# A hybrid decoder layer on one Trainium2 core: eight operand sums of the second token half moved into the up-projection, the output weight ring in other memory, the first up operands prepared earlier

## The chip, the core and the metric

The kernel runs on one core of one Trainium2 chip. TensorE multiplies (PE in the profile; its weight loads are PEld), VectorE (DVE) and ScalarE (ACT) do elementwise work, GpSimd (POOL) and SyncE (SP) mostly issue DMAs. The metric is the device time of one execution in microseconds, the median of several. Lower is better.

## The reference

One layer, 2048 tokens of width 1024, all in float32. Two token mixers (a gated linear recurrence and an RWKV-7 recurrence) make the rows of `o`; they are untouched by the change. What follows them is:

```
x = x + concat(o_hg, o_rw) @ w_out            # 1024 x 1024
h = rmsnorm(x, norm2_w)
u = h @ w_up                                  # 1024 x 5632
u = causal_depthwise_conv(u, conv_w, width 3) + conv_b
gate, val = split(u)                          # 2816 each
x = x + (silu(gate) * val) @ w_down           # 2816 x 1024
out = rmsnorm(x, final_norm_w)
```

## The kernel before

**Precision and products.** Every float32 operand is split into a high part (a cast by ScalarE, line 237 or 244) and a low part (a subtraction by DVE, line 238 or 245), and one product is three matmuls (`mm3`, lines 260 to 262). The up- and the down-projection each use a scheme with seven block products instead of eight. Its price is that sums and differences of operand blocks have to be made.

**Stages.** Phase 1 does the input projection, the mixers, and the output projection of the token blocks 0 to 2 (512 tokens each). What the change touches comes behind it.

*Output projection of block 3* (lines 1144 to 1219). For two column halves `dh` there are eight steps; a step multiplies one 128-row part of `o` (`take`, operand parts in `Bh[3]`, `Bl[3]`, `Bh[5]`, `Bl[5]`) by one piece of `w_out` (`weights`). The split weights go into a ring of three `woh` and three `wol` tiles. `xh` holds the residual rows of x, four tiles for each `dh` in a ring of six; DVE adds the product to them (line 1218) and SP stores them to `x1d`. In the second half the moving operands 0, 1 and 4 of the up-projection are built beside it (`build`), and its first weights `A0` are loaded. The pool `op` that holds these tiles is opened when phase 1 has given its memory back, so its tiles lie where tiles of phase 1 lay; `yo`, the last result of the RWKV heads, is stored to DRAM by POOL out of such memory.

*Up-projection* (`run`, line 1324). The loop runs over 2 x 22 iterations: token half h (1024 tokens, two blocks), then 22 column blocks. An iteration multiplies seven operands made of the weight quarters a11, a12, a21, a22 by seven moving operands B0 to B6, each product being 12 matmuls: a11 with B0, then (`late`) a22 with B6 and s4 with B2 of the iteration before, then a12 with B1, s2 with B4, s1 with B3, s3 with B5, where s1 = a21 + a22, s2 = s1 - a11, s3 = a11 - a21, s4 = a12 - s2. In iteration 0 the operand parts B3, B5, B6 and B2 are still built, four `build` calls ahead of the product before. Behind the seven products the convolution, SiLU and multiplication make `y`, which SP stores to `gd_` (line 1423): blocks 0 and 1 in half 0, blocks 2 and 3 in half 1.

*Work aside.* A list `side` holds small pieces of other work; after every product `aside(n)` takes one (line 1290). In half 0 these are the second norm of the blocks 2 and 3 and the operand sums for half 1 and for `w_down`; in half 1 the sums for the down-projection of the tokens of half 0: for each of 11 row blocks kk, four loads of `gd_`, four DVE operations (`s_make`), four stores to `Sg[0]`. `four` makes the pieces, with pauses (`None`) in which the loads land. They use the ring `br` of six tiles.

*Down-projection* (lines 1429 to 1519). 143 steps, for each token half g seven products of 11 row blocks (one product of half 0 is made beside the up-projection). A step loads two tiles `draw`, splits them, and does 12 matmuls. The same sums for the second token half (`g_sums`, into `Sg[1]`) are made here: `sums_at` spreads the eleven over the steps 13, 18, 23 to 63. Their first use is at step 88.

**What sets the order.** The program is one list; a scheduler places each engine's instructions by priority and by its own estimate of when operands are ready. On the chip each engine, and SP with its DMA issues, then runs its list strictly in order, each instruction waiting on semaphores. So whatever stands behind a waiting instruction on the same engine waits too.

Of the kernel before, what the change touches and what calls it, by code (L numbers as in the profile page):

```python
# [61 lines left out]
def tile_layer(ctx, tc, consts, x, norm1_w, w_in, hg_lb_logits, hg_norm_w, rw_shift_mu, rw_w0, rw_w2,  # L62
# [1044 lines left out]
    with ExitStack() as c2:  # L1107
# [11 lines left out]
        def raw_(src):  # L1119
            t_ = hr.tile([P, BLK], F32, tag="br", name="br", bufs=6)  # L1120
            if src is not None:
                loader[0](t_, src)
            return t_
# [20 lines left out]
        with tc.tile_pool(name="op", bufs=1, reuse_waits="tile") as op_:  # L1144
# [43 lines left out]
                return wh, wl  # L1188

            xt = {}  # L1190
            for dh in range(2):
                accs = [pst("wacc") for _ in range(4)]
                for n, k in enumerate((0, 1, 4, 5, 2, 3, 6, 7)):
                    w = weights(k, dh)
                    if dh == 0:
                        take(k)
                    if n == 5:
                        for i in range(4):
                            t0 = b * BLK + i * P
                            xt[i] = op_.tile([P, 512], F32, tag="xh", name="xh", bufs=6)  # L1200
                            load(xt[i], x[0, t0:t0 + P, dh * 512:dh * 512 + 512])
                    if dh == 0 and n == 6:
                        rows_of_conv()
                    if dh == 1 and n == 4:
                        for i, (lo_, hi_) in enumerate(((0, 88), (88, 176))):
                            vps = pst("cps")
                            TE.transpose(vps[:, 0:88], crow[i], ident[0:88, 0:88])
                            V.tensor_copy(cvt[:, lo_:hi_], vps[:, 0:88])
                        A0 = up_raw(0)
                    if dh == 1 and 2 <= n:  # L1210
                        for j in range(2):
                            q = 2 * (n - 2) + j
                            build(0, (0, 1, 4)[q // 4], q % 4)
                    for i in range(4):
                        is_ = slice(i * P, (i + 1) * P)
                        mm3(accs[i], (ohl[k][0][:, is_], ohl[k][1][:, is_]), w, n == 0, n == KD - 1)
                for i in range(4):
                    V.tensor_add(xt[i], accs[i], xt[i])
                    dma(x1d[b][i * P:(i + 1) * P, dh * 512:dh * 512 + 512], xt[i])


        with tc.tile_pool(name="up", bufs=1, reuse_waits="tile") as up:
# [2 lines left out]
            V.memset(halo, 0.0)  # L1225


            side = []

            def norm_last(b, i2):  # L1230

                xt = []

                def load():
                    for q in range(2):
                        xt.append(up.tile([P, D], F32, tag="xt2", name="xt2", bufs=2))
# [11 lines left out]
                side.extend([load, None, lambda: scale(0), lambda: scale(1), None] + [lambda: next(g)] * KD)  # L1248

            def four(srcs, make, dsts):  # L1250

                ts = []
                side.extend([lambda: ts.extend(raw_(v) for v in srcs), None,
                             lambda: make(ts, 0), lambda: (make(ts, 1), [dma(d, t_) for d, t_ in dsts(ts)]), None])

            def t_make(ts, part):
                b11, b12, b21, b22 = ts
# [30 lines left out]
            late_side = len(side) - late_side  # L1288
# [18 lines left out]
            def between():  # L1307

                accs = [pst("fa") for _ in range(4)]
                for kk in range(KH):  # L1310
                    lhs, rhs = (split(uw, raw_(v), [P, BLK], "uw", 5)
                                for v in (krows(gd_[0], 1, kk), wd_quarter(1, 0, kk)))
                    for i in range(4):
                        mm3(accs[i], [t_[:, i * P:(i + 1) * P] for t_ in lhs], rhs, kk == 0, kk == KH - 1, True)
                    if kk == KH - 1:
                        break
                    yield
                for i in range(4):
                    t_ = raw_(None)
                    act(t_, accs[i], AF.Copy)  # L1320
                    dma(M2[i], t_)
                yield

            def run():
                fill_ = between()
# [8 lines left out]
                for n in range(2 * NFF + 1):  # L1334
                    h, fb = n // NFF, n % NFF
                    if n < 2 * NFF:
# [42 lines left out]
                    operand("a12", a12)  # L1379
                    prod(acc_b, "a12", 1, True)  # L1380
                    V.tensor_add(cg[:, 2:2 + BLK], acc_b, m1)
                    s1 = up.tile([P, 4, P], F32, tag="s1", name="s1", bufs=1)
                    s2 = up.tile([P, 4, P], F32, tag="s2", name="s2", bufs=1)
                    V.tensor_add(s1, a21, a22)
                    V.tensor_sub(s2, s1, a11)
                    operand("s2", s2)
                    prod(acc_a, "s2", 4, False)
                    m2 = part(acc_a, "m2")
                    operand("s1", s1)
# [39 lines left out]
    with tc.tile_pool(name="dn", bufs=1, reuse_waits="tile") as dn:  # L1429
# [121 lines left out]
```

## Time and profile before

| | |
|---|---|
| median of 3 timed runs | 2756.31 us (2747.66 to 2756.97) |
| the profiled execution | 2742.4 us |
| its span in the profile | 2740.6 us |
| granted TensorE clock | 0.989 of full |
| TensorE busy | 2638.4 us |
| VectorE busy | 1899.1 us |
| ScalarE busy | 1349.5 us |
| read from HBM / written | 376.27 MB / 138.41 MB |
| weight pieces for the up-projection | 176 DMAs of 256 KB |

In the profile, a row of a timeline gives the start, the length, the engine (SPq is the queue of DMA issues of SyncE), the line, the operation and its tiles, a count when equal instructions were merged, and in brackets how long the engine idled before and on whom it waited. A row of waits reads: who waited, for whom, microseconds in total, how many times, the longest. Matmuls overlap, so a 128x512 matmul is shown with about 0.39 us though the next one starts sooner. The input projection and the mixers take the first 1380 us, the output projection of block 3 goes on to 1431, the up-projection to 2331, and the rest is the down-projection.

### The profile page before, as it was taken

The page shows a single profiled execution, that of the slowest core. Times are in us where ns is not written, and L with a number is a line of the kernel's source. Part 1 is how long each engine was busy: PE and PEld are TensorE (multiplying, and loading weights), DVE is VectorE, ACT ScalarE, POOL GpSimd, SP SyncE. Part 2 cuts the span into 40 slices and gives each one's busy share as a digit, 9 for nine tenths or more (in the row PEclk, how much of TensorE's full clock was granted, in tenths as well). Part 3 has the DMA queues.
Part 4 walks back from the last instruction along what each step waited for, and adds up shares of the span by engine and source line. Part 5 has one row for each costly group of instructions (what it writes and reads, how often), then busy time and mean ns, then how long its engine had stood idle before and what let it go on. Part 6 is the DMA issues. An engine that isn't in the chain of part 4 may idle for free.

```text
span 2740.6 us, 47945 instructions
## 1 busy us (share of the span) xinstructions
PE 2638.4 (96%) x18059; PEld 2098.8 (77%) x18059; DVE 1899.1 (69%) x3665; ACT 1349.5 (49%) x2168; POOL 368.9 (13%) x660
## 2 busy tenths in 40 slices
PE   7999999989999999999899999999999999998998
PEld 6777777767777767778677888887888888776887
DVE  4857656575456664757568789988898787667656
ACT  5455443444544444443356754556445554445544
POOL 6433222212222113222100000000000000000000
PEclk9999999999999999999999999999999999999999
DMA  8655544355653546933674467746763222999865
GB/s 303 199 166 166 165 136 130 117 148 183 214 167 111 148 152 204 311 123 119 182 265 139 140 199 258 240 148 207 264 232 113 90 86 76 323 333 327 298 194 184
DMA packets 365437, 517.87 MB, mean 189 GB/s; under 512 B 97439, under 2 KB 194069, under 8 KB 365205
## 3 DMA queue, kind: packets, MB, share of 16 engines
q1 hardware_dynamic: 313265, 345.39, 38.9%
q0 software_dynamic: 51872, 169.41, 19.0%
q8 instruction: 142, 2.33, 0.4%
q14 instruction: 90, 0.74, 0.1%
q10 hardware_dynamic: 68, 0.02, 0.0%
HBM read 376.27 MB, written 138.41 MB: 188 GB/s over the span
## 4 chain that ended last, share of the span: by engine, by line
PE 68%; DMA 10%; DVE 8%; issue 6%; ACT 5%; SPq 1%; POOL 1%; DVEq 0%; ACTq 0%; POOLq 0%
PE pj L260 8%; PE pj L261 7%; PE pj L262 7%; PE ua L262 5%; PE ua L260 5%; PE ua L261 5%; PE ud L262 2%; PE ud L260 2%; PE ud L261 2%; PE da L261 2%; PE da L260 2%; PE da L262 2%; PE hg L971 2%; DMA woraw<-in_w_out_dram 2%; PE ub L262 1%
## 5 line engine op out<-in xcount | busy, mean ns | idle before, releaser
L260 PE MATMUL pj<-hh,wh 128*128 128x512 f32 x960 | 403.5, 420 | 1.4 <-ACT hh L117 0.7
L261 PE MATMUL pj<-hl,wh 128*128 128x512 f32 x960 | 379.5, 396 | 0.0
L262 PE MATMUL pj<-hh,wl 128*128 128x512 f32 x960 | 379.2, 395 | 0.0
L260 PE MATMUL ua<-Bh,uwh 128*128 128x512 f32 x704 | 276.8, 393 | 4.9 <-ACT uwh L244 3.1
L262 PE MATMUL ua<-Bh,uwl 128*128 128x512 f32 x704 | 275.1, 391 | 0.2 <-DVE uwl L245 0.2
L261 PE MATMUL ua<-Bl,uwh 128*128 128x512 f32 x704 | 274.7, 390 | 0.0
L260 PEld LDWEIGHTS pj<-hh,wh 128*128 128x128 f32 x960 | 181.7, 189 | 54.7 <-issue 11.8
L261 PEld LDWEIGHTS pj<-hl,wh 128*128 128x128 f32 x960 | 182.0, 190 | 39.4 <-issue 6.2
L262 PEld LDWEIGHTS pj<-hh,wl 128*128 128x128 f32 x960 | 181.6, 189 | 39.8 <-issue 0.4
L244 ACT CAST uwh<-uraw 128x512 fp32r<-128x512 f32 x220 | 134.1, 617 | 124.6 <-PE ua L261 58.5
L245 DVE TENSOR_TENSOR uwl<-uraw,uwh 128x512 fp32r<-128x512 f32 x220 | 147.0, 686 | 48.7 <-ACT uwh L244 48.5
L244 ACT CAST dah<-draw 128x512 fp32r<-128x512 f32 x140 | 87.0, 622 | 184.7 <-DMA draw<-Sg 60.0
L245 DVE TENSOR_TENSOR dal<-draw,dah 128x512 fp32r<-128x512 f32 x140 | 96.6, 690 | 103.8 <-ACT dah L244 103.5
L260 PEld LDWEIGHTS ua<-Bh,uwh 128*128 128x128 f32 x704 | 132.6, 188 | 33.6 <-ACT uwh L244 3.5
L262 PEld LDWEIGHTS ua<-Bh,uwl 128*128 128x128 f32 x704 | 132.5, 188 | 28.4 <-DVE uwl L245 0.6
L261 PEld LDWEIGHTS ua<-Bl,uwh 128*128 128x128 f32 x704 | 132.7, 188 | 27.0
L260 PE MATMUL ud<-Bh,uwh 128*128 128x512 f32 x352 | 137.9, 392 | 0.3 <-ACT uwh L244 0.3
L262 PE MATMUL ud<-Bh,uwl 128*128 128x512 f32 x352 | 137.1, 390 | 0.0
L261 PE MATMUL ud<-Bl,uwh 128*128 128x512 f32 x352 | 137.0, 389 | 0.0
L261 PE MATMUL da<-dbl,dah 128*128 128x512 f32 x340 | 133.3, 392 | 1.3 <-DVE dbl L245 1.3
L262 PE MATMUL da<-dbh,dal 128*128 128x512 f32 x340 | 132.3, 390 | 0.0
L260 PE MATMUL da<-dbh,dah 128*128 128x512 f32 x340 | 124.6, 392 | 6.5 <-ACT dbh L244 6.5
(570 smaller groups left out, 6050.3 us busy)
## 6 DMA issues: line engine op xcount, KB each, us to landing
uraw<-in_w_up_dram SPq DMA_DIRECT2D x176, 256.0 KB, 3.4
woraw<-in_w_out_dram POOLq DMA_DIRECT2D x96, 256.0 KB, 3.5
draw<-Sg SPq DMA_DIRECT2D x88, 256.0 KB, 3.4
draw<-Tw SPq DMA_DIRECT2D x88, 256.0 KB, 3.4
gd<-y SPq DMA_DIRECT2D x86, 256.0 KB, 3.0
xt<-x1d SPq DMA_DIRECT2D x32, 512.0 KB, 7.2
wraw<-in_w_in_dram POOLq DMA_DIRECT2D x60, 256.0 KB, 4.7
br<-in_w_down_dram SPq DMA_DIRECT2D x58, 256.0 KB, 3.8
```

What stands on the lines that cost most here:

```text
L244: S.copy(hi, src)
L245: V.tensor_sub(lo, src, hi.bitcast(F32))
L260: TE.matmul(acc, lh, rh, start=first, stop=False, skip_group_check=skip)
L261: TE.matmul(acc, lh, rl, start=False, stop=False, skip_group_check=skip)
L262: TE.matmul(acc, ll, rh, start=False, stop=last, skip_group_check=skip)
L971: TE.matmul(o, kt[:, t0:t0 + 64], qs, start=True, stop=True, tile_position=(0, e * 64))
```

## The change

Three edits.

1. *Sums of the second token half.* The list `side` now carries with each piece the first iteration at which it may be taken. Behind the eleven sums of half 0, whose pieces now become free one sum an iteration from iteration 23 on, come the first eight (`EARLY`) of the second half: sum kk from iteration 35 + kk on, the one in which the rows it needs have just been stored. In the down-projection three sums remain, at the steps 13, 19 and 25.
2. *The output weight ring.* The four first `xh` tiles are allocated ahead of the ring, and `xh` gets eight buffers instead of six. The ring `woh`, `wol` so comes to lie in other memory, and `xh` where it lay.
3. *The first up operands.* In iteration 0 a12, s2 and s1 are made and split right behind a11, ahead of the building of B3, B5, B6 and B2. `s1` and `s2` move from the pool `up`, which follows `op` in the same memory, to the pool `uw`.

```diff
+    EARLY = 8
...
+            def x_tile(i):
+                xt[i] = op_.tile([P, 512], F32, tag="xh", name="xh", bufs=8)
+
+            for i in range(4):
+                x_tile(i)
             for dh in range(2):
...
-                            xt[i] = op_.tile([P, 512], F32, tag="xh", name="xh", bufs=6)
+                            if dh:
+                                x_tile(i)
...
-            side = []
+            side, first_at = [], [1]
+
+            def aside_of(fs):
+
+                side.extend((first_at[0], f) for f in fs)
...
-            late_side = len(side)
-            for kk in range(KH):
-                four([krows(gd_[u], q, kk) for u, q in QB], s_make, s_out(lambda i, kk=kk: krows(Sg[0][i], 0, kk)))
+            for g in range(2):
+                for kk in range(({0: KH, 1: EARLY})[g]):
+                    first_at[0] = NFF + 1 + g * (KH + 1 + kk)
+                    four([krows(gd_[2 * g + u], q, kk) for u, q in QB], s_make,
+                         s_out(lambda i, g=g, kk=kk: krows(Sg[g][i], 0, kk)))
...
-                if side and (1 <= n < NFF - 2 or n > NFF) and (n > NFF or len(side) > late_side):
-                    f = side.pop()
+                if side and n >= side[-1][0] and not NFF - 2 <= n <= NFF:
+                    f = side.pop()[1]
...
+            def weight_sums(a11, a21, a22):
+
+                s1, s2 = (uw.tile([P, 4, P], F32, tag=nm, name=nm, bufs=1) for nm in ("s1", "s2"))
+                V.tensor_add(s1, a21, a22)
+                V.tensor_sub(s2, s1, a11)
+                return s1, s2
...
                         if n == 0:
+                            operand("a12", a12)
+                            s1, s2 = weight_sums(a11, a21, a22)
+                            operand("s2", s2)
+                            operand("s1", s1)
                             for kk in range(4):
                                 build(0, 3, kk)
...
-        sums_at = {KH + 5 * j + 2: j for j in range(KH)}
+        sums_at = {KH + 6 * j + 2: EARLY + j for j in range(KH - EARLY)}
```

The line numbers of the changed kernel are one higher from line 181 on, and more further down. How the instructions stand, at three places:

ScalarE's list where the output projection of block 3 begins, before; `uraw` holds the loaded pieces, `woh` are the split weights, `Bh` the operand parts, and the brackets name the semaphores that an instruction waits for (DMASW is a queue of POOL, DMAHW one of SP):

```order
L237 CAST woh<-uraw 128x512 [waits DMAHW0_49,DVE_49]
L237 CAST woh<-uraw 128x512 [waits DMASW0_49,DVE_49,Activation_49]
L237 CAST woh<-uraw 128x512 [waits DMAHW0_49]
L237 CAST Bh_14661<-uraw 128x512 [waits PE_49]
L237 CAST Bh_14661<-uraw 128x512
L237 CAST Bh_14664<-uraw 128x512 [waits DMAHW1_49]
```

and now:

```order
L238 CAST woh<-uraw 128x512 [waits DMAHW0_49]
L238 CAST woh<-uraw 128x512
L238 CAST woh<-uraw 128x512 [waits DMAHW0_49]
L238 CAST Bh_14661<-uraw 128x512 [waits PE_49]
L238 CAST Bh_14661<-uraw 128x512
L238 CAST Bh_14664<-uraw 128x512 [waits DMAHW1_49,DVE_49]
```

The order is the same. The second `woh` no longer waits for a queue of POOL and for DVE; the wait for TensorE ahead of the first `Bh` stays.

ScalarE's list from the last steps of the output projection to the first iteration of the up-projection, before; `uwh` are the split weight operands (from `s` for s1 and s2, from `uraw` otherwise), Bh_14653 and _14654 the parts of B1 and B4, Bh_14661, _14664, _14658 and _15084 those of B3, B5, B6 and B2, `m` a product that is kept:

```order
L237 CAST woh<-Bl_14657 128x512
L237 CAST Bh_14654<-br 128x512 x2
L237 CAST Bh_14661<-br 128x512 x4
L237 CAST Bh_14664<-br 128x512 x4
L117 ACTIVATE m_15137<-ua 128x512
L237 CAST Bh_14658<-br 128x512 x2
L244 CAST uwh<-s_15177 128x512
L237 CAST Bh_14658<-br 128x512
L244 CAST uwh<-s_15176 128x512
L237 CAST Bh_14658<-br 128x512
L237 CAST Bh_15084<-br 128x512 x4
```

The same place now, first the weight pieces of the output projection and then what begins the up-projection:

```order
L238 CAST Bh_14653<-br 128x512 x2
L245 CAST uwh<-s_15098 128x512
L245 CAST uwh<-s_15097 128x512
L245 CAST uwh<-uraw 128x512
L238 CAST woh<-Bl_14657 128x512
```

```order
L238 CAST Bh_14661<-br 128x512 x4
L238 CAST Bh_14664<-br 128x512 x4
L117 ACTIVATE m_15153<-ua 128x512
L238 CAST Bh_14658<-br 128x512 x4
L117 ACTIVATE m_15216<-ua 128x512
L238 CAST Bh_15084<-br 128x512 x4
L245 CAST uwh<-uraw 128x512 x4
```

The casts of s2, s1 and s3 moved ahead of the last three weight pieces of the output projection and of all parts of B3, B5, B6 and B2; behind B2's parts now comes a11 of iteration 1.

SP's list in one of the last iterations of the up-projection, where before there are only the two stores of `y` and four `uraw` loads; now (gd_156 and gd_157 are the blocks 2 and 3, Sg_162 to _165 the sums of the second token half):

```order
L1447 DMA gd_156<-y_22394 128x512
L1447 DMA gd_157<-y_22394 128x512
L1140 DMA uraw<-in_w_up_dram 128x4x128
L1123 DMA br<-gd_156 128x512
L1123 DMA br<-gd_157 128x512 x2
L1140 DMA uraw<-in_w_up_dram 128x4x128
L1123 DMA br<-gd_156 128x512
L1266 DMA Sg_162<-br 128x512
L1266 DMA Sg_164<-br 128x512
L1266 DMA Sg_163<-br 128x512
L1140 DMA uraw<-in_w_up_dram 128x4x128
L1266 DMA Sg_165<-br 128x512
```

And SP's list in the down-projection, as one sum stood there before, eleven times over:

```order
L1436 DMA sraw<-gd_156 128x512 x2
L1436 DMA sraw<-gd_157 128x512 x2
L1436 DMA draw<-Sg_158 128x512
L1436 DMA draw<-Tw_166 128x512
L1436 DMA draw<-Sg_158 128x512
L1436 DMA draw<-Tw_166 128x512
L199 DMA Sg_162<-sraw 128x512
L199 DMA Sg_163<-sraw 128x512
L199 DMA Sg_164<-sraw 128x512
L199 DMA Sg_165<-sraw 128x512
```

The loads of `gd` moved from among the `draw` loads to right behind the stores that write them, with one `uraw` load between; three sums stay as they stood.

More of the change, by code (lines that the diff above doesn't have):

```diff
@@ L1247, in norm_last @@
                 g = transposed(xt, "n2", lambda: pst("tp"), evict)
-                side.extend([load, None, lambda: scale(0), lambda: scale(1), None] + [lambda: next(g)] * KD)
+                aside_of([load, None, lambda: scale(0), lambda: scale(1), None] + [lambda: next(g)] * KD)
             def four(srcs, make, dsts):
                 ts = []
-                side.extend([lambda: ts.extend(raw_(v) for v in srcs), None,
-                             lambda: make(ts, 0), lambda: (make(ts, 1), [dma(d, t_) for d, t_ in dsts(ts)]), None])
+                aside_of([lambda: ts.extend(raw_(v) for v in srcs), None,
+                          lambda: make(ts, 0), lambda: (make(ts, 1), [dma(d, t_) for d, t_ in dsts(ts)]), None])
             def t_make(ts, part):
@@ L1283, in tile_layer @@
                 four([wd_quarter(q, dh, kk) for q, dh in QB], t_make, t_out(lambda i, kk=kk: krows(Tw[i], 0, kk)))
-            late_side = len(side)
-            for kk in range(KH):
-                four([krows(gd_[u], q, kk) for u, q in QB], s_make, s_out(lambda i, kk=kk: krows(Sg[0][i], 0, kk)))
+            for g in range(2):
[3 more added lines that the diff above has]
+                         s_out(lambda i, g=g, kk=kk: krows(Sg[g][i], 0, kk)))
             side.reverse()
-            late_side = len(side) - late_side
             def aside(n):
-                if side and (1 <= n < NFF - 2 or n > NFF) and (n > NFF or len(side) > late_side):
-                    f = side.pop()
+                if side and n >= side[-1][0] and not NFF - 2 <= n <= NFF:
+                    f = side.pop()[1]
                     if f is not None:
@@ L1378, in run @@
                     acc_b, acc_d = pst("ub"), pst("ud")
-                    operand("a12", a12)
+                    if n:
+                        operand("a12", a12)
                     prod(acc_b, "a12", 1, True)
                     V.tensor_add(cg[:, 2:2 + BLK], acc_b, m1)
[L1382 to L1386, printed above, removed]
+                    if n:
+                        s1, s2 = weight_sums(a11, a21, a22)
+                        operand("s2", s2)
                     prod(acc_a, "s2", 4, False)
                     m2 = part(acc_a, "m2")
-                    operand("s1", s1)
+                    if n:
+                        operand("s1", s1)
                     prod(acc_d, "s1", 3, True)
```

## Prediction

> **What bounds the kernel now.** I read the page first, then the idle time of TensorE, then the stretches that hold it.
>
> ```profile
> PE 2638.4 (96%) x18059; PEld 2098.8 (77%) x18059; DVE 1899.1 (69%) x3665; ACT 1349.5 (49%) x2168; POOL 368.9 (13%) x660
> PE   7999999989999999999899999999999999998998
> DMA  8655544355653546933674467746763222999865
> 1421.73 0.39 PE L260 MATMUL wacc<-woh,Bh 128*128 128x512 f32 x1
> 1431.03 0.39 PE L262 MATMUL wacc<-woh,Bl 128*128 128x512 f32 x1
> ```
>
> TensorE is busy 96% of the span, so only its waits can be won. Undisturbed it starts a 128x512 matmul every 0.227 us (41 of them between the two starts in the last rows). I count a loss as time beyond that pitch, because a "busy" matmul at a slow clock also loses. The second row of digits is the DMA: 9 in the slices from 2329 to 2535 us, the first half of the down-projection, and 2 to 3 in the four slices before, the end of the up-projection. The change moves work across that border. The stretches show what it costs there (columns: length, busy time and instructions of PE, PEld, DVE, ACT, POOL, then clock, DMA share, GB/s):
>
> ```profile
> 2330.00:2405.00 75.00, 71.24 (x308) 57.17 (x308) 50.95 (x79) 34.85 (x56) 1.11 (x2) 1.00 0.91 327
> 2405.00:2545.00 140.00, 130.11 (x546) 101.71 (x545) 97.78 (x147) 66.28 (x122) 0.00 (x0) 0.99 0.94 334
> 2580.00:2720.00 140.00, 140.00 (x619) 115.95 (x618) 81.41 (x125) 63.38 (x118) 0.00 (x0) 1.00 0.64 204
> ACT dah L244 <- DMA draw<-Sg: 56.5, 24, 5.0
> ACT dah L244 <- DMA draw<-gd: 25.3, 9, 5.8
> ACT dah L244 <- PE da L261: 48.9, 31, 1.6
> ```
>
> Both stretches of 140 us run the same steps (two loads, two splits, twelve matmuls). The one from 2580 fits 619 matmuls, the one from 2405 only 546: 73 missing, times 0.227, is **16.5 us**. The waits name the reason: between 2360 and 2545 ScalarE's splits wait 82 us for loads of `draw` (first two rows of waits); from 2580 to 2700 they wait for TensorE alone (last row). At 334 GB/s and a share of 0.94 the DMA is what is full.
>
> **Part C: eight of eleven `g_sums` of the second half leave the down-projection.**
>
> ```profile
> L1436 SPq DMA_DIRECT2D sraw<-gd x44: 319/424/1168, 2362.2 to 2515.9; - x44
> sraw<-gd SPq DMA_DIRECT2D x44, 256.0 KB, 5.1
> ```
>
> A sum is four loads and four stores of 256 KB. Eight sums are 64 DMAs, 16.8 MB, that is 50 us of DMA time at 334 GB/s. The loads of the eleven are now issued from 2362 to 2516 us, at every fifth step from 13 to 63. The three that stay come at steps 13, 19 and 25: twelve steps of 2.72 us (12 x 0.227) behind 2362 is 2395, and with their stores they are through by about 2405. Ahead of that they are hardly thinner than before, so the loss of the stretch 2330 to 2405 stays: 308 matmuls against 331 is 5 us. Of the 16.5 us behind it all but the part of the finishing goes: the output stores and `xt` loads of half 0 fall into the same stretch, and I leave 1.5 us for them, though those of half 1 cost nothing in the stretch from 2580. **C = 15 us**; bounds 8 (half of the loss belongs to finishing and SP's order) and 17.5.
>
> **Part D: the same eight sums in the last up iterations.** Per sum this adds eight DMAs on SP and four DVE operations.
>
> ```profile
> 1900.00:2100.00 200.00, 200.00 (x883) 165.36 (x882) 176.99 (x263) 101.38 (x151) 0.00 (x0) 1.00 0.64 212
> 2130.00:2330.00 200.00, 200.00 (x882) 165.10 (x881) 152.10 (x211) 101.24 (x145) 0.00 (x0) 1.00 0.25 81
> L1122 SPq DMA_DIRECT2D br<-gd x44: 319/382/682, 1919.8 to 2061.5; - x44
> L1268 DVE TENSOR_TENSOR br<-br x11: 682/690/693, 1925.1 to 2052.4; 128x512 f32<-128x512 f32 x11
> ```
>
> The first stretch already holds eleven such sums (rows three and four), 1.4 an iteration, with DVE at 177 of 200 us and TensorE at 200 of 200. After the change there is one an iteration in both; DVE in the second goes from 152 to 152 + 32 x 0.69 = 174 us, below the row that costs nothing. **D = 0**. What hides it is DVE's remaining 26 us and the splits' lead on TensorE; the price when that is gone is in the rival below. Above: the sums of the first half are only spread out, which can win nothing where TensorE loses nothing.
>
> **Part A: the ring of split output weights.** TensorE's longest single wait behind phase 1:
>
> ```profile
> 1380.02 0.39 PE L262 MATMUL pj<-wh,hl 128*128 128x512 f32 x1
> 1382.84 1.14 ACT L237 CAST woh<-uraw 128x512 fp32r<-128x512 f32 x2 [4.93 <-DMA oT<-yo]
> 1383.88 1.66 ACT L237 CAST Bh<-uraw 128x512 fp32r<-128x512 f32 x3
> 1384.55 0.80 PE L260 MATMUL wacc<-woh,Bh 128*128 128x512 f32 x1 [4.15 <-ACT Bh L237]
> 1388.85 0.62 ACT L237 CAST Bh<-Bh 128x512 fp32r<-128x512 f32 x1 [0.75 <-DMA Bh<-oT]
> 1390.90 0.40 PE L260 MATMUL wacc<-woh,Bh 128*128 128x512 f32 x1
> ```
>
> ScalarE may write the second `woh` only when the store of `yo` has left that memory, and the operand casts `Bh` queue behind it. From 1380.25, when the next matmul was due, to 1390.90 there are 15 matmuls, 3.4 us of work in 10.65: a loss of 7.2 us, 4.3 in the wait and the rest at 0.43 us a matmul behind it. Now no `woh` waits for a queue of POOL; the `Bh` cast still waits for the last `pj` matmuls, so TensorE starts 0.67 us (1383.88 to 1384.55) after 1380.4. Next late is the fourth weight: its cast stands behind the `Bh` cast that waits for a load until 1388.85, so it is done near 1390.0, and TensorE wants it at 1381.1 + 36 x 0.227 = 1389.3. Remaining loss 0.85 + 0.75, win 5.6 us at this place.
>
> **Part B: the first up operands.**
>
> ```profile
> 1436.47 0.39 PE L262 MATMUL ub<-Bh,uwl 128*128 128x512 f32 x1
> 1438.07 1.28 ACT L237 CAST Bh<-br 128x512 fp32r<-128x512 f32 x2 [3.29 <-DMA br<-Ts]
> 1439.25 0.61 ACT L244 CAST uwh<-s 128x512 fp32r<-128x512 f32 x1
> 1439.92 0.50 PE L260 MATMUL ua<-Bh,uwh 128*128 128x512 f32 x1 [3.06 <-ACT uwh L244]
> 1443.73 0.62 ACT L237 CAST Bh<-br 128x512 fp32r<-128x512 f32 x1 [0.74 <-DMA br<-h2d]
> 1441.01 0.98 SPq L1139 DMA_DIRECT2D uraw<-in_w_up_dram  x2
> 1450.87 0.39 PE L260 MATMUL ua<-Bh,uwh 128*128 128x512 f32 x1
> 1390.00:1441.00 51.00, 47.63 (x210) 38.74 (x208) 33.63 (x58) 26.20 (x45) 0.00 (x0) 0.99 0.88 294
> ```
>
> The cast of `s2` sits behind operand parts whose loads are late. From 1436.70 to 1450.87, where iteration 1 begins, there are 36 matmuls, 8.2 us of work in 14.2: a loss of 6.0 us. With `s2`, `s1` and `s3` split early, those 36 run through. Next late is iteration 1's own a11: its cast stands behind the last operand part (1443.73) and its load (issued at 1441.01, 3.4 to land by the page's row quoted below, then a cast of 0.6), so it is ready near 1445.2 if the loads come when they come now: a win of 5.6 us for A and B together. If the loads move up by all of A's 5.6 us, it is 11.2. They can move up only as far as the DMA lets them: 0.88 of 51 us is 45 us of transfers, and at the 0.94 above that takes 48, so about 3 to 3.5 us. **A + B = 9 us**, bounds 5 and 11. The price of seven DVE and three ACT operations pulled ahead of the dh = 1 matmuls (some 7 us on engines with 17 and 25 free of 51) is inside the lower bound. Two more `xh` buffers let x loads go without waiting for stores; I give that nothing.
>
> A clock rule bears on A and B.
>
> ```profile
> 2378.55 1.20 PE L260 MATMUL da<-dbh,dah 128*128 128x512 f32 x4 [1.73 <-ACT dbh L244]
> 2508.50 0.96 PE L260 MATMUL db<-dbh,dah 128*128 128x512 f32 x3 [2.63 <-ACT dbh L244]
> 2511.48 0.63 PE L261 MATMUL db<-dbl,dah 128*128 128x512 f32 x1
> ```
>
> Behind 1.73 us of idling the rows go on at full pitch; behind 2.63 us, with a second wait of 1.00 close to it, matmuls take 0.63 instead of 0.39 us. So the remaining waits of under a microsecond in A cost only themselves. The Trainium skill (TensorE: Matmul & The Clock Gate, Part 1) puts the fall to half rate after an idle window of about 3.4 us; the trace disagrees here, with the slow rows behind 2.63 and 3.06 us. By the page B would win up to 2.9 us less (its 6.0 without the wait of 3.06); the sum goes by the rows.
>
> **Sum.** 15 + 0 + 9 = 24 us. The profiled execution took 2742.4 us (span 2740.6, 1.8 around it), so the same execution would take 2718. It lies 13.9 us below the median of the three timed runs, 2756.31, and 5 below the fastest; I know no reason and take the difference over: **2732 us**.
>
> **Rivals.**
>
> *H, half of it.* A + B stay bound by loads (5 us), and in C the waits belong to finishing and SP's order (8 to 10): about 15 us, time 2741. For it: the DMA share of 0.88 in A and B, and the wait at 2508 near the output stores. Against: the stretch from 2580 with no sums and no loss, though it loads and stores `xt` too.
>
> *L, a new loop in the up-projection*, which ends on the other side. A sum now reads `gd` rows that SP stored one iteration before.
>
> ```profile
> 2198.55 1.23 DVE L1421 TENSOR_TENSOR y<-y,y 128x1024 f32<-128x1024 f32 x1
> 2199.81 0.82 SPq L1423 DMA_DIRECT2D gd<-y  x2
> gd<-y SPq DMA_DIRECT2D x86, 256.0 KB, 3.0
> uraw<-in_w_up_dram SPq DMA_DIRECT2D x176, 256.0 KB, 3.4
> 2205.31 0.69 DVE L245 TENSOR_TENSOR uwl<-s,uwh 128x512 fp32r<-128x512 f32 x1 [1.16 <-ACT uwh L244]
> 2217.55 0.39 PE L260 MATMUL ud<-Bh,uwh 128*128 128x512 f32 x1
> ```
>
> On SP the `br` loads stand one load behind that store, and behind them the next `uraw` loads; on DVE the sums stand behind the split at 2205.31. The store lands 3.0 us behind 2199.8, the loads are issued in 0.8 and land in 3.4 (the row of `uraw`, the nearest of that size): about 2207, or 7.2 us behind the end of `y` at 2199.78. Then come four sums (2.5 us), and the rest of what DVE does in an iteration: 152.1 / 200 of 19.05 us (84 x 0.227) is 14.5, less the 5.1 it is busy from 2199.78 to the split's end at 2206.00, is 9.4. The loop is 19.1 us: it just fits an iteration. The splits run ahead, too: the one that ends at 2206.0 is used at 2217.55, 11.5 us later. With landings of 5.1 us, as `sraw` had, the loop is 22.9, and eight iterations lose 8 x 3.85 - 11.5 = 19 us: time 2751, no net change. It decides from a loop of 23.5 us on, where all 24 us are given back; at 25.3 the kernel is 14 us slower, 2770 us. Against: a DMA share of 0.25 there. The Trainium skill (DMA: Bandwidth & Descriptors, Rules for kernel authors) has the reading DMA wait for the first one's completion before it is issued, which is the order assumed here; no row of before has such a pair this close.
>
> **How the numbers follow.** The forecast (20 to 30 us) 0.60, H (14 to 20) 0.22, L up to no net change 0.13, L beyond it 0.05. A measurement of this kernel can tell about 0.5%, 13.8 us, from no change. So faster 0.82, same 0.13, slower 0.05. The range: at the low end A + B + C at their upper bounds, 28.5 us, and 10 us for runs that fall as low as the profiled one did, 2718; at the high end H's smallest win less some of L, 10 us, 2746.
>
> **What would show it.** C: no `draw` waits of ScalarE worth naming behind 2400 us, 32 more `br<-gd` in the up-projection and `sraw` x12, and the stretch after 2405 with about 4.4 matmuls a microsecond. D: TensorE at 100% in the second up half. A: no 4 us idle before the first `wacc`. B: the three products after `ub` without idling, then a short wait for a11 of iteration 1. The prediction is wrong if TensorE waits for `uwl` or `uwh` late in the up-projection (L), or if the down-projection still waits for `draw` after its last `sraw` load (H).

## The result, and the profile after

| | before | changed |
|---|---|---|
| median | 2756.76 us (8 runs) | 2740.42 us (8 runs, 2734.07 to 2744.7) |
| ratio, 95% interval | | 0.9938 [0.9922, 0.9954] |
| the profiled execution | 2742.4 us | 2740.67 us |
| last `pj` matmul of phase 1 starts at | 1380.02 us | 1390.39 us |

The change makes the kernel about 0.6% faster, 16 us by the medians. A second measurement of it, beside other kernels (below), gave 0.9954 [0.9938, 0.9970], 14 us. The forecast was 24 us and 2732 us.

The two profiled spans differ by 1.7 us only. That is phase 1, which the change doesn't touch: its last matmul came at 1380.02 us in the profile of before and at 1385.6 to 1398.4 us in the twelve other profiles of this study. So stretches behind phase 1 are compared here, not spans. From that matmul to the end it is 2740.6 - 1380.0 = 1360.6 us before and 2738.9 - 1390.4 = 1348.5 us now, 12.1 us less.

The page of the changed kernel, for the rows shown of before:

```profile
PE 2634.9 (96%) x18059; PEld 2098.9 (77%) x18059; DVE 1896.9 (69%) x3665; ACT 1344.5 (49%) x2168; POOL 367.4 (13%) x660
PE   7999999989999999999899999999999999999998
DMA  8655544355663546844575357746763454888665
```

The DMA digits of the last up iterations went from 3, 2, 2, 2 to 3, 4, 5, 4, and the 9, 9, 9, 8 behind them to 8, 8, 8, 6: the transfers have moved. The stretches of the same kernel (length, busy time and count of PE, PEld, DVE, ACT, POOL, then clock, DMA share, GB/s):

```profile
1900.00:2100.00 200.00, 197.93 (x871) 163.00 (x870) 177.15 (x263) 100.98 (x151) 0.00 (x0) 1.00 0.63 207
2130.00:2330.00 200.00, 192.89 (x844) 157.50 (x843) 166.19 (x241) 95.63 (x140) 0.00 (x0) 1.00 0.50 164
2330.00:2405.00 75.00, 71.12 (x308) 57.15 (x307) 48.35 (x71) 34.26 (x53) 1.10 (x2) 1.00 0.83 290
2405.00:2545.00 140.00, 139.83 (x616) 114.98 (x615) 94.27 (x141) 75.19 (x142) 0.00 (x0) 1.00 0.85 286
```

In the last stretch 616 matmuls instead of 546: 70 x 0.227 = 15.9 us won. The stretch before it holds 308, as before. But the second up half, which had 882 matmuls and no loss, now has 844: 38 x 0.227 = **8.6 us lost**. The forecast had 0 there. (The first row, from 1900, has 12 matmuls fewer than before. That is for the most part one wait of 1.91 us at the turn of the two halves, ending at 1902.87; before had it too, 1.57 us, but ending at 1898.27, outside the stretch.) The waits of the second up half say where (who waited, for whom, us in total, times, longest):

```profile
ACT y L117 <- DVE cg L1431: 36.6, 10, 5.7
DVE br L1280 <- DMA br<-gd: 24.3, 8, 3.9
ACT uwh L245 <- DVE s L1341: 19.5, 8, 2.7
PE ua L261 <- ACT m L117: 7.1, 6, 1.6
```

DVE waits for the loads of all eight sums, 3.0 us each. ScalarE then waits for DVE (`cg` is `u` of the gate ahead of the convolution), and TensorE for `m`, a copy of the product `ua` that ScalarE makes out of PSUM, where the products of TensorE stand. One iteration in time order, from the timelines of DVE, SP, ScalarE and TensorE:

```profile
2268.61 1.23 DVE L1445 TENSOR_TENSOR y<-y,y 128x1024 f32<-128x1024 f32 x1
2269.86 0.82 SPq L1447 DMA_DIRECT2D gd<-y  x2
...
2271.73 0.62 ACT L245 CAST uwh<-s 128x512 fp32r<-128x512 f32 x1 [2.65 <-DVE s L1341]
2272.25 0.59 ACT L117 ACTIVATE m<-ua 128x512 f32<-128x512 f32 x1
...
2272.74 1.88 SPq L1123 DMA_DIRECT2D br<-gd  x4
2272.90 0.50 PE L261 MATMUL ua<-Bh,uwh 128*128 128x512 f32 x1 [1.60 <-ACT m L117]
...
2278.70 0.69 DVE L1280 TENSOR_TENSOR br<-br 128x512 f32<-128x512 f32 x1 [3.92 <-DMA br<-gd]
2289.04 1.22 DVE L1445 TENSOR_TENSOR y<-y,y 128x1024 f32<-128x1024 f32 x1
```

Read it as a loop. `y` is stored at 2269.86, the loads of the sum follow at 2272.74, DVE stands at the sum until 2278.70, and everything behind it in DVE's list (convolution, the next `y`, the next `s`) comes late. ScalarE's cast `uwh<-s` waits for `s`; the copy `m` stands behind that cast, and TensorE may not go on in that PSUM bank before `m` is out.

The border of phase 1, from the timelines of TensorE, DVE and ScalarE, and behind them the stretch that holds it (PE busy 7.55 us with 25 matmuls; the clock is the third number from the end):

```profile
1390.39 0.39 PE L263 MATMUL pj<-wh,hl 128*128 128x512 f32 x1
1390.61 0.40 PE L261 MATMUL wacc<-woh,Bh 128*128 128x512 f32 x1
1392.16 0.50 PE L262 MATMUL wacc<-wol,Bh 128*128 128x512 f32 x1 [1.15 <-DVE wol L239]
1393.96 0.62 PE L263 MATMUL wacc<-woh,Bl 128*128 128x512 f32 x1 [1.30 <-DVE Bl L239]
1396.95 0.63 PE L261 MATMUL wacc<-woh,Bh 128*128 128x512 f32 x1
...
1390.13 1.37 DVE L401 TENSOR_TENSOR xh<-pj,xh 128x512 f32<-128x512 f32 x2 [0.79 <-PE pj L263]
1391.42 1.89 DVE L239 TENSOR_TENSOR wol<-uraw,woh 128x512 fp32r<-128x512 f32 x3
1393.22 1.89 DVE L239 TENSOR_TENSOR Bl<-uraw,Bh 128x512 fp32r<-128x512 f32 x3
...
1389.22 1.66 ACT L238 CAST Bh<-uraw 128x512 fp32r<-128x512 f32 x3
```

```profile
1390.00:1400.00 10.00, 7.55 (x25) 5.49 (x24) 5.67 (x9) 2.13 (x5) 0.63 (x1) 0.83 0.85 282
```

The wait of 4.15 us is gone: the operand casts `Bh` start at 1389.22, ahead of the last `pj`, and the first `wacc` follows it without a gap. In its place TensorE waits twice for low parts, which DVE makes only behind two additions that wait for those last `pj` matmuls themselves. Behind the two waits matmuls take 0.63 us, and the granted clock of these 10 us is 0.83.

Iteration 0 of the up-projection: between the products no wait is left but the one that the prediction named as next, iteration 1's own a11, in TensorE's and ScalarE's timelines:

```profile
1453.81 0.50 PE L261 MATMUL ua<-Bh,uwh 128*128 128x512 f32 x1 [1.01 <-ACT uwh L245]
1453.13 2.25 ACT L245 CAST uwh<-uraw 128x512 fp32r<-128x512 f32 x4 [0.38 <-DMA uraw<-in_w_up_dram]
```

### The profile page after: what moved, and what is told of

It is laid out like the page before. It is cut to its first block, busy times and chain, and to the rows that moved or that the text cites. A ratio compares the mean times of both kernels' runs of the same rounds, so it can differ in the third digit from the quotient of the medians.

```text
span 2738.9 us, 47949 instructions
## 1 busy us (share of the span) xinstructions
PE 2634.9 (96%) x18059; PEld 2098.9 (77%) x18059; DVE 1896.9 (69%) x3665; ACT 1344.5 (49%) x2168; POOL 367.4 (13%) x660
## 4 chain that ended last, share of the span: by engine, by line
PE 67%; DMA 10%; DVE 10%; issue 6%; ACT 4%; SPq 1%; POOL 1%; DVEq 0%; ACTq 0%; POOLq 0%
PE pj L261 8%; PE pj L262 7%; PE pj L263 7%; PE ua L261 4%; PE ua L263 4%; PE ua L262 4%; PE da L262 2%; PE da L261 2%; PE da L263 2%; PE ud L263 2%; PE ud L261 2%; PE ud L262 2%; PE db L262 2%; PE db L263 2%; PE hg L972 2%
## 5 line engine op out<-in xcount | busy, mean ns | idle before, releaser
L261 PE MATMUL da<-dbh,dah 128*128 128x512 f32 x340 | 131.2, 390 | 3.4 <-ACT dbh L245 3.4
```

The lines of the kernel that those rows point to most:

```text
L261: TE.matmul(acc, lh, rh, start=first, stop=False, skip_group_check=skip)
```

## The experiments

For each kernel the table gives the ratio to before, the start of the last `pj` matmul, and what TensorE lost at four places. For the border (last `pj` to 8 us behind the first `wacc`), iteration 0 and the start of the down-projection (distances that end in 2330 to 2420 us) I added, over TensorE's timeline, what each distance between the starts of two matmuls has above 0.227 us. For the second up half (2130 to 2330) and the stretch 2405 to 2545 I counted the missing matmuls, against 882 and 619, times 0.227.

| kernel | ratio to before, 95% | last `pj` | border | iter. 0 | up half | start | 2405 on |
|---|---|---|---|---|---|---|---|
| before | 1 | 1380.0 | 7.2 | 5.8 | 0 | 5.7 | 16.5 |
| changed | 0.9938 [0.9922, 0.9954] | 1390.4 | 4.6 | 1.6 | 8.6 | 5.8 | 0.7 |
| changed_again | 0.9954 [0.9938, 0.9970] | 1389.7 | 4.5 | 0.2 | 8.6 | 7.9 | 0 |
| sums_only | 0.9970 [0.9957, 0.9983] | 1394.8 | 6.3 | 6.6 | 7.3 | 8.1 | 3.0 |
| ring_only | 0.9995 [0.9981, 1.0008] | 1398.4 | 4.6 | 6.7 | 0 | 6.9 | 15.7 |
| early_only | 0.9985 [0.9970, 1.0001] | 1390.7 | 7.2 | 0.9 | 0 | 7.8 | 13.4 |
| early_ring | 0.9972 [0.9959, 0.9985] | 1392.2 | 4.5 | 3.9 | 0 | 6.4 | 16.6 |
| delay | 0.9942 [0.9919, 0.9965] | 1389.9 | 4.5 | 1.0 | 9.1 | 7.5 | 0.7 |
| hold | 0.9927 [0.9908, 0.9947] | 1395.0 | 3.0 | 2.4 | 5.4 | 7.5 | 1.1 |
| old_rows | 0.9904 [0.9879, 0.9930] | 1395.9 | 4.6 | 1.5 | 0 | 4.6 | 0 |
| behind | 0.9908 [0.9888, 0.9927] | 1385.6 | 4.6 | 1.8 | 0 | 7.9 | 0 |
| behind_9 | 0.9910 [0.9887, 0.9933] | 1392.9 | 4.6 | 1.3 | 0 | 7.5 | 0 |
| behind_late | 0.9905 [0.9880, 0.9931] | 1389.1 | 4.5 | 0.9 | 0 | 4.0 | 0 |

The intervals reach 4 to 7 us to either side, and phase 1 alone moves a profile by up to 18 us, so the places tell the kernels apart better than the ratios do. Programs are not laid at the same microsecond in each profile, so the two fixed stretches carry a few matmuls of uncertainty; sums_only, which runs 12 us behind the changed kernel there, shows in the last column what belongs to the start.

The places aren't all that varies behind phase 1. From the last `pj` to the end of the span it is 1360.6 us in before, 1348.5 and 1350.1 in the two profiles of the changed kernel, 1350.8 in delay, 1346.1 in hold, 1340.8 in behind, 1339.9 in behind_9, 1337.3 in behind_late and 1337.4 in old_rows; and 1357.9 in sums_only, 1363.0 in ring_only, 1364.2 in early_only, 1357.8 in early_ring. One profile each, so a few us either way are not told apart; by this measure ring_only and early_only aren't shorter than before at all.

### The three parts alone

*sums_only*: edit 1 on the kernel before.

> Only the eight sums are moved; the weight ring and the first up operands stay as before. Theory W (the sums win 15 us in the down-projection and give about 7.6 back in the last up iterations, where DVE waits for rows stored just before): 2756.8 - 7.5 = about 2749 us, ratio 0.997; TensorE loses 8 to 10 us between 1905 and 2330 and under 1 us in the 140 us stretch of the down-projection that lost 15.5. By the prediction's own Part D at 0: 2742, ratio 0.9945.

Measured 0.9970, 2750.32 us against 2758.08: 8 us won, near what theory W gives, not the 15 of part D at 0. The gain in the down-projection comes with a loss of 7.3 us in the second up half.

*ring_only*: edit 2 alone.

> Only the memory of the weight ring is changed. By the prediction's Part A: no wait of 4 us ahead of the first wacc, 5.6 us won there, but the loads of the up-projection's first operands are bound by the DMA, so that 3 to 5.6 us remain: ratio 0.998 to 0.999, 2751 to 2754 us. Rival: the win at this place is spent again in iteration 0 (B's loss grows from 5.8 to 9): ratio 0.9995 to 1.0.

Measured 0.9995, 2756.83 us against 2758.08: no difference can be told. At the border 2.6 us are won, not 5.6, and iteration 0 loses 0.9 us more.

*early_only*: edit 3 alone.

> Only the first up operands are prepared earlier. By the prediction's Part B: 5 to 6 us won in iteration 0, since A's wait still stands ahead and the loads have their time: ratio 0.998, 2751 us. Rival: the loss goes to a11 of iteration 1, whose load comes behind the operand parts: 2 us or less, ratio 0.9993 or more.

Measured 0.9985, 2754.23 us, 4 us. Iteration 0 loses 0.9 instead of 5.8 us: the forecast of 5 to 6 holds at that place. The interval allows it, and no change too.

*early_ring*: both, and the sums as before.

> Ring and early operands together, the sums as before. The prediction's A + B: 9 us, ratio 0.9967, 2749 us. By the stretches of the changed kernel (TensorE loses 4.6 us at the border of phase 1 instead of 7.3, and 1.6 in iteration 0 instead of 5.8): 7 us, ratio 0.9975, 2751 us. If the two parts add up as measured alone: 5 us, 0.998.

Measured 0.9972, 2750.9 us: 7 us. With the 8 us of sums_only that is 15 us, what the whole change gives; by the medians, and within their intervals, the parts add up. The profiles don't show it as well: in that of early_ring the border and iteration 0 lose 8.4 us, 4.6 less than before, since iteration 0 still waits 1.73 us for a11 of iteration 1, with slow matmuls behind the wait.

### Why the sums cost time in the up-projection

First theory W: DVE waits for rows that were stored just before. Rival V: DVE has too much to do, 166 of 200 us. *delay* takes each of the eight sums one iteration later:

```diff
-                    first_at[0] = NFF + 1 + g * (KH + 1 + kk)
+                    first_at[0] = NFF + 1 + g * (KH + 2 + kk)
```

> The changed kernel, with each of the eight sums taken one iteration (19 us) later, so that the stores that it reads are long done; the same loads, DVE work and stores in the same part of the program. Theory W (DVE and what queues behind it wait for rows stored just before): TensorE loses under 3 us between 1905 and 2330 instead of 9.7, and the time is 7 us below the changed kernel: ratio 0.991, 2732 us. Rival V (DVE has too much to do, 166 of 200 us): the loss of 9.7 stays within 2 us, ratio 0.994, 2740 us.

Measured 0.9942; the up half loses 9.1 us, as in the changed kernel. By its expectation that speaks for V. But the timelines of SP and DVE show that the experiment had not done what I meant:

```profile
2271.16 0.81 SPq L1447 DMA_DIRECT2D gd<-y  x2
...
2275.46 0.32 SPq L1123 DMA_DIRECT2D br<-gd  x1
...
2282.69 0.69 DVE L1280 TENSOR_TENSOR br<-br 128x512 f32<-128x512 f32 x1 [4.80 <-DMA br<-gd]
...
2156.91 0.69 DVE L1280 TENSOR_TENSOR br<-br 128x512 f32<-128x512 f32 x1 [2.81 <-DMA br<-gd]
```

The loads still come 4 us behind a store of `y`, and DVE still waits. The first of the eight sums (last row) starts at 2156.91 us, as in the changed kernel (2156.75), and not an iteration of 19 us later: the scheduler had pulled the later loads up again, to right behind the stores. `first_at` says when a piece is recorded, not when it runs. So three kernels were made that hold the order in other ways.

*old_rows*: as many loads and sums, of the first half's rows, stored long before. So its output isn't the layer's; it serves for the time alone.

```diff
-                    four([krows(gd_[2 * g + u], q, kk) for u, q in QB], s_make,
+                    four([krows(gd_[u], q, kk) for u, q in QB], s_make,
```

> The eight sums read rows of the first token half, stored long before, instead of their own (so the second half's Sg holds other numbers); same count of loads, DVE operations and stores in the same iterations. The run before this one, with the sums one iteration later in the program, still had each load right behind the store of its own row on SP, since the scheduler pulled it up to there; so it left theory W untested. Theory W (DVE meets the sum before its loads have landed, because they wait for the store of their rows): DVE's waits for br fall from 24 us to under 8, TensorE loses under 4 us between 1905 and 2330 instead of 9.7, ratio 0.991 to 0.992. Rival V (DVE simply has 166 us of work in 200): the loss stays at 8 or more, ratio 0.994.

*hold*: the loads ordered on SP behind the store of the next row (`stored` collects the stores of `y`).

```diff
-                    first_at[0] = NFF + 1 + g * (KH + 1 + kk)
+                    first_at[0] = NFF + 1 + g * (KH + 2 + kk)
...
+                        i_ = dma(t_, v)
+                        if g1:
+                            tc.add_manual_dep(i_.ins, stored[-1].ins.name, NOSYNC, reason="behind the next row")
```

> The changed kernel, where a sum's four loads stand on SP behind the store of the next row, so that the rows which they read were stored an iteration (19 us) before and no load waits for a store to land; DVE's order is the same as in the changed kernel. Theory W: the loads are issued 2 to 3 us sooner against DVE's list, its waits for br fall from 24 us to about 8, TensorE loses 2 to 5 us in the second up half instead of 9; ratio 0.992. Rival V: the loss stays at 8 or more, ratio 0.994.

*behind*: the loads where they were, and the first two operations of each sum ordered on DVE behind the multiplication that ends `y`.

```diff
-                    V.tensor_add(a22, a21, a22)
-                    V.tensor_sub(a21, a11, a21)
+                    i_ = V.tensor_add(a22, a21, a22)
+                    if g1:
+                        tc.add_manual_dep(i_.ins, last_y[-1].ins.name, NOSYNC, reason="behind y")
+                    i_ = V.tensor_sub(a21, a11, a21)
+                    if g1:
+                        tc.add_manual_dep(i_.ins, last_y[-1].ins.name, NOSYNC, reason="behind y")
...
-                        V.tensor_mul(ys[0], ys[0], ys[1])
+                        last_y.append(V.tensor_mul(ys[0], ys[0], ys[1]))
```

> The changed kernel, where DVE makes each of the eight sums behind the multiplication that ends y, some 12 us later in its list; the loads still stand right behind the store. Theory W: DVE has no wait for br, cg and the casts' sums come on time, TensorE loses under 2 us in the second up half instead of 9; ratio 0.991. Rival V: DVE has the same work, the loss stays at 8 or more. Rival X: the sums' stores now stand ahead of the next loads, which wait for their buffers, and the weight loads behind these on SP come late: waits of ScalarE or DVE for uraw, loss 5 or more.

The second up half of the three, first old_rows, where the scheduler pulled the sums ahead, so that five of the eight lie in that stretch; the second row has all eight:

```profile
2130.00:2330.00 200.00, 200.00 (x883) 165.44 (x882) 165.90 (x238) 100.79 (x146) 0.00 (x0) 1.00 0.41 134
2080.00:2232.00 152.00, 151.83 (x671) 125.36 (x669) 139.29 (x204) 78.37 (x114) 0.00 (x0) 1.00 0.59 196
```

As long a stretch of the changed kernel, with its eight sums but for the end of the last:

```profile
2148.00:2300.00 152.00, 147.31 (x645) 120.39 (x644) 126.20 (x187) 72.04 (x106) 0.00 (x0) 1.00 0.57 186
```

hold, and behind it, from its waits in that stretch, DVE's for the loads:

```profile
2130.00:2330.00 200.00, 195.52 (x858) 160.22 (x857) 169.42 (x246) 97.46 (x143) 0.00 (x0) 1.00 0.52 166
```

```profile
DVE br L1290 <- DMA br<-gd: 16.6, 7, 4.1
DVE br L1290 <- issue: 3.4, 1, 3.4
```

behind, and then `y` and the first operation of a sum in its timeline of DVE:

```profile
2130.00:2330.00 200.00, 200.00 (x883) 165.12 (x881) 170.64 (x243) 101.92 (x145) 0.00 (x0) 1.00 0.52 171
```

```profile
2255.69 1.23 DVE L1450 TENSOR_TENSOR y<-y,y 128x1024 f32<-128x1024 f32 x1
2256.83 0.69 DVE L1281 TENSOR_TENSOR br<-br 128x512 f32<-128x512 f32 x1
2274.73 1.23 DVE L1450 TENSOR_TENSOR y<-y,y 128x1024 f32<-128x1024 f32 x1
2275.87 0.69 DVE L1281 TENSOR_TENSOR br<-br 128x512 f32<-128x512 f32 x1
```

In old_rows DVE is busy 139.3 of the 152 us with the eight sums, more than the 126.2 in the changed kernel, and TensorE does 671 matmuls there against 645: V falls. DVE waits for no load of a sum. In behind DVE is even busier than in the changed kernel (170.6 of 200 us against 166.2, since TensorE gets more done), with all eight sums in the stretch, and TensorE is full again. The loads come even later there, 3.4 to 6.9 us behind the store of `y` (store 2161.74, loads 2165.17 to 2168.69), since three stores of the sum just made go ahead of them; but DVE comes to the sum only 12 us behind them (2180.67). The load on the DMA isn't the difference either: its share is 0.50 in the changed kernel and 0.52 in behind.

hold is the weaker proof. The loads no longer wait for a store to land, the loss falls by three eighths (5.4 instead of 8.6 us), but DVE still waits 20.0 us at the eight sums (16.6, and 3.4 in the row that names the issue) instead of 24.3, where 8 were expected. From the end of `y` to the sum it is 7.7 us in the mean instead of 8.5. So the landing of the store is a small part of it; four loads that SP issues right behind `y` are late for DVE's place whatever rows they read.

So W holds in a wider form than it was put: the loss came from DVE's place in front of data that were still on the way, be it behind a store or behind their own late issue. Rival X, late weight loads, did not show: in the second up half of behind neither DVE nor ScalarE waits for `uraw`.

### A better version

`changed_again` is the changed kernel once more; `behind_9` and `behind_late` are behind with one edit each:

```diff
-    EARLY = 8
+    EARLY = 9
```

```diff
-        sums_at = {KH + 6 * j + 2: EARLY + j for j in range(KH - EARLY)}
+        sums_at = {KH + 12 * j + 32: EARLY + j for j in range(KH - EARLY)}
```

> The changed kernel once more, on the chip of the two that follow: ratio 0.994 as before, 2741 us; TensorE loses 8 to 10 us in the second up half.

> The sums behind y, nine of them instead of eight, so that two stay in the down-projection. Theory W: a ninth sum in the up-projection costs TensorE nothing there (DVE about 172 of 200 us, no loss in the second up half), and its 8 DMAs leave the first steps of the down-projection, which lose 5 to 8 us now: 0 to 2 us better than eight behind y, ratio 0.990 to 0.991. Rival V: over 1 us lost in the second up half.

> The sums behind y, and the three that stay in the down-projection at the steps 43, 55 and 67 instead of 13, 19 and 25. If the 5 to 8 us that TensorE loses in the first 90 us of the down-projection are due to these sums' DMAs: 3 to 5 us better than eight behind y, ratio 0.989 to 0.990. If they are due to the start itself (draw loads behind SP's order, whole operand pairs): the loss stays, and some is added behind 2420; ratio 0.991.

Medians: 2742.58, 2732.49 and 2729.63 us. The ninth sum costs nothing in the up-projection and wins nothing that can be told in the start of the down-projection. Later steps for the three sums that stay win something there: of the waits for a split `dbh` the last one, 47 us behind the first (1.48 us long at 2392.97 in the changed kernel, 1.0 to 2.5 us in the other profiles), is the one that is missing in behind_late, and nothing is added behind 2420. It cost 1.6 us in the changed kernel, and 3.9 in behind, where slow matmuls follow it (the start loses 7.9 us there and 4.0 in behind_late); 3 to 5 us had been expected. The scheduler pulled these loads ahead too: the first is issued at 2389.52 us, 26 us later than in behind (2363.39), where the edit asks for 30 steps of 2.72 us. The rest of the loss, 4.0 us, belongs to the start itself. By the ratio behind_late (0.9905) can't be told from behind (0.9908); its median is the lowest of all, 27 us below before and 13 below the changed kernel in the same comparison. The two intervals, [0.9880, 0.9931] and [0.9938, 0.9970], don't overlap.

## Why the prediction was right, and where it failed

*Time.* 2732 us were forecast, in 2718 to 2746; 2740 came, in the range and on the right side, by the size of rival H (14 to 20 us). But H's reason didn't come: C was whole. The range held since its high end had left room for some of L, not because every term was right; 2732 itself was missed by 8 us.

*Part C, right.* 15 us forecast, 15.9 by the count of matmuls. ScalarE's waits for `draw<-Sg` and `draw<-gd` between 2400 and 2545 still are 17 us in 9 waits (63.6 in 24 before, from 2405), so the sign "no `draw` waits of ScalarE worth naming behind 2400 us" didn't come as written; but they no longer reach TensorE, which is busy 139.83 of 140 us. The loss ahead of it stayed, as said (5.7, now 5.8 us). Some 2 to 4 us of it are the remaining sums' doing, by behind_late.

*Part D, the step that failed.* "D = 0. What hides it is DVE's remaining 26 us and the splits' lead on TensorE." Neither hid it. It cost 8.6 us, the largest part of what the forecast was off: A, B and C together won 6.9 + 15.9 = 22.8 us in the profile, near the 24 of the sum. (With the loss that makes 14.2 us; it is 12.1 by the stretches behind phase 1 and 16 by the medians.) The 26 us are an average, and a free engine doesn't help where its list stands at data that are still on the way. The row taken as the proof, 1900 to 2100 us with DVE at 177 us and no loss, has sums of rows stored long before; old_rows is that case in the second half, and costs nothing either. So load was measured, and order was the question.

Rival L had this mechanism, with the chance 0.13 on "no net change" and the price put too far off. Its loop was 7.2 us from the end of `y` to the sum, 2.5 of sums and 9.4 of other work, 19.1 us. The changed kernel shows, from DVE's timeline:

```profile
2146.56 1.23 DVE L1445 TENSOR_TENSOR y<-y,y 128x1024 f32<-128x1024 f32 x1
2156.75 0.69 DVE L1280 TENSOR_TENSOR br<-br 128x512 f32<-128x512 f32 x1 [2.74 <-DMA br<-gd]
...
2309.71 1.22 DVE L1445 TENSOR_TENSOR y<-y,y 128x1024 f32<-128x1024 f32 x1
```

From `y` to `y` it is (2309.71 - 2146.56) / 8 = 20.4 us, and 19.04 in behind. The first leg is 8.96 us in these rows and 8.5 in the mean of the eight; the rest, 20.4 - 8.5 = 11.9 us, is what the prediction had (2.5 + 9.4). So one term was short by 1.3 us: in the iteration shown above the four loads were issued over 1.88 us, not 0.8, and DVE could go on 4.1 us behind the end of that (2274.62 to 2278.70), not 3.4. Eight turns that are 1.35 us too long make 10.8 us, and TensorE lost 8.6. The second error was the cover: the lead of 11.5 us was read from a split, but TensorE was stopped by the copy `m`, which has no such lead. So the sign given for L, TensorE waiting for `uwl` or `uwh`, was the wrong one to look for: in the second up half no such wait is there. By these figures about 2 us of lead were there.

*Part A, right in kind, half in size.* 5.6 us forecast, 2.6 won. The wait for the store of `yo` went, and even the 0.67 us expected behind `pj`. What was missed is DVE: the low parts of the first weight and operand stand behind two additions that wait for the last `pj`, 1.15 and 1.30 us, and a slow clock behind them, 8 matmuls by 0.2 us (granted clock 0.83 over those 10 us). The sentence that the remaining waits "cost only themselves" failed with it.

*Part B, right.* 6.0 us lost before, 1.6 now, and the wait left is the one named, a11 of iteration 1. A and B together won 6.9 us (13.1 to 6.2) in the profile, inside 5 to 11, though not the 9 taken; early_ring has 7 us by its ratio. Single profiles scatter here: with both edits iteration 0 loses from 0.2 us (changed_again) to 3.9 (early_ring). That it was the DMA that bounded the sum was not shown: what fell short was DVE at the border.

*The base.* That the profiled execution lay 13.9 us below the median was carried over unexplained. The profiles put most of it down to phase 1 (the column of the last `pj`): over the thirteen, the profiled execution goes from 14.4 us below its kernel's median, where the last `pj` starts earliest (before, 1380.0), to 6.3 above it, where it starts latest (ring_only, 1398.4). So it was right to make the sum against that execution and to add the difference.

*The clock rule.* The prediction set the Trainium skill's idle window of about 3.4 us (TensorE: Matmul & The Clock Gate, Part 1) against slow rows behind 2.63 and 3.06 us. Those rows stand; a still shorter case is below.

## What to carry to other kernels

When work is moved beside a busy engine, the engine's spare time is not enough to know: ask where in the list of each in-order engine the moved instruction stands, what it waits for there, and what stands behind it. A loop from a store through a load back to the same engine is priced from its legs, each by its own row, and compared with the period; if it is as long as the period, put the consumer behind the work that feeds the next turn (behind: 19.04 instead of 20.4 us). And an experiment that delays something in the program delays nothing if a scheduler may pull it forward; look at the order before reading the time.

## What was not expected of the hardware

The same two waits of TensorE, 1.15 and 1.30 us with one matmul between, were followed by a slow clock in the changed kernel and by none in hold. There, from TensorE's timeline, and the 10 us around it:

```profile
1396.73 0.50 PE L262 MATMUL wacc<-wol,Bh 128*128 128x512 f32 x1 [1.15 <-DVE wol L239]
1398.54 0.50 PE L263 MATMUL wacc<-woh,Bl 128*128 128x512 f32 x1 [1.30 <-DVE Bl L239]
1398.88 0.40 PE L261 MATMUL wacc<-woh,Bh 128*128 128x512 f32 x1
```

```profile
1394.60:1404.60 10.00, 7.55 (x32) 5.65 (x31) 5.67 (x9) 1.98 (x4) 0.60 (x1) 1.00 0.86 282
```

The granted clock is 1.00 here and 0.83 in the changed kernel, and 25 matmuls became 32. The Trainium skill (TensorE: Matmul & The Clock Gate, Part 1) calls its window of activity free-running. That fits two waits which sometimes slow the clock and sometimes don't, though neither is near 3.4 us, nor is their sum; no run here shows the window itself. hold is the exception: of the ten kernels with the moved ring, the other nine lost 4.5 or 4.6 us at the border, hold 3.0.

Phase 1, the same in every kernel here, ended 18 us apart from profile to profile (1380.0 to 1398.4 us). What in it varies stays open.
